# Seven groups instead of four take the first k tile, three of them leave PSUM in turn, and constant matmuls fill two pauses of TensorE

## The chip, the cores and the metric

The kernel runs on one core of a Trainium2 chip. The metric is device time in microseconds (us), and less is better. A profiled execution gives beside its time a span, from the first to the last instruction. The engines are PE (TensorE; PEld is its loading of stationary operands), DVE (VectorE), ACT (ScalarE), POOL (GpSimd) and SP (SyncE, which here issues the weight transfers). Each engine works through its own instructions in a fixed order.

## What is computed

One decoder layer for 256 tokens of width 2048, in float32, with weights that are read once:

```
mod = silu(c) W_ada + b_ada -> shift1, scale1, gate1, shift2, scale2, gate2
h   = RMSNorm(x)(1+scale1)+shift1
p   = h W_in, columns split into [retention q,k,v,g | HGRN2 q,f,i,g | gate A | gate B]
yA  = W_retO( LN_head(Retention(rope(q),rope(k),v)) * silu(g) )
yB  = W_hgO( RMS_head(HGRN2(silu(q), f, i)) * silu(g) )
x   = x + gate1 * ( (sigmoid(gA)*yA + sigmoid(gB)*yB) W_out )
h2  = RMSNorm(x)(1+scale2)+shift2
[a, b] = split(causal_depthwise_conv3(h2 W_up))
out = RMSNorm_final( x + gate2 * ( (silu(a) * b) W_down ) )
```

The change touches the beginning alone: the norm of x, `scale1` and `shift1`, and the first 12 column groups of `p = h W_in`.

## The kernel before

**Products in three parts.** A float32 weight is split into a rounded upper part `wh` (ACT, line 167) and the rest `wl` (DVE, `raw - wh`, line 172), and so are the activations `hT` (the first half of a tile is the upper part, from ACT, line 345; the second half is the rest, from DVE, line 350). PE multiplies upper by upper, upper by rest and rest by upper. There are 12 groups g of 512 columns (`wa[g]`) and 16 k tiles of 128 rows. In this text a **unit** is one k tile of one group: a piece of 128x512 weights, for PE 12 matmuls of 256 columns (`mm_cols`, lines 209 to 211), or 6 of 512 columns (`mm_rows`, lines 196 to 198; groups 4, 5, 10, 11). The whole loop has 192 units. Two units can come in one transfer of 128x1024, and are then split in one instruction each of ACT and DVE.

**The activations come k tile by k tile.** `ada[k]` is a generator that makes `hT` of one k tile: four transfers of `ada1` (0.5 MB each), four dot products on DVE (`ada_dot`, line 398), then the small ACT steps (409, 410, 412), and `modulated`, which writes `hT`. So a group can only be multiplied with the k tiles that are there, and the loop goes round the groups several times. At each visit of a group `have` says how many k tiles there are to be:

```python
have = min(KT, 2 + int((work - LAG) / ADA_EVERY))
```

`work` counts the units that are traced, `ADA_EVERY` is 11.

**PSUM.** Groups 0 and 1 (`RESIDENT`) stay in PSUM (`po` buffers) until they are done. Any other group gets one of two `pg` buffers for a visit, and then leaves it: `take` copies it out with ACT at the group's first visit (`fresh`, line 743), and adds it to what is there with DVE at each later one (line 745). A `pg` buffer is free for the visit after next once that is done.

**Order.** DMA, ACT and DVE instructions of the opening are pinned to the order of the code (`pin`); later the framework orders them, and `pump` mixes in the generators: queue 1 with the `ada` tiles, queue 0 with the HGRN2 and retention work as soon as its groups are done. SP issues the weights in order into 12 `raw` buffers; `wh` and `wl` have four buffers each.

**The beginning.** PE broadcasts `c` (line 259) for its silu, sums the squares of x (`token_rstd`, line 298: matmuls with one column), waits for `1/rms`, broadcasts that (line 312) into `rx`, and waits until the first `hT` is there. Then groups 0 to 3 take k tile 0, and after four more dots k tile 1; groups 2 and 3 leave PSUM, and the loop goes on with group 4.

Of the kernel before, what the change touches and what calls it, by code (L numbers as in the profile page):

```python
# [14 lines left out]
BF16 = mybir.dt.bfloat16  # L15
I32 = mybir.dt.int32
AF = mybir.ActivationFunctionType
ALU = mybir.AluOpType

P = 128  # L20
# [9 lines left out]
G = 512  # L30
NORM_EPS = 1e-6
HEAD_EPS = 1e-5
FIRST = 4
RESIDENT = 2
ADA_EVERY = 11
LAG = 1
NOSYNC = mybir.DependencyInfo(mybir.DependencyClass.NoSync, mybir.DependencyReason.DATA)
SMALL = 70

# [16 lines left out]
class Kernel:  # L56
# [181 lines left out]
    def constants(self):  # L238
        nc, a, c = self.nc, self.a, self.consts
        self.ones = c.tile([P, P], F32, name="ones")  # L240
        nc.vector.memset(self.ones, 1.0)
        self.eps1 = c.tile([P, 1], F32, name="eps1")
        nc.vector.memset(self.eps1, NORM_EPS)
        self.eps2 = c.tile([P, 1], F32, name="eps2")
        nc.vector.memset(self.eps2, HEAD_EPS)
        self.halfpi = c.tile([P, 1], F32, name="halfpi")
        nc.vector.memset(self.halfpi, math.pi / 2)

        self.silu = []
        self.sc = c.tile([P, D + 1], F32, name="sc")  # L250
        nc.vector.memset(self.sc[:, D:], 1.0)
        rows = [self.blk([1, GW], name="crow") for _ in range(2)]
        for u, row in enumerate(rows):
            nc.scalar.dma_start(out=row, in_=a["c"][:, u * GW : (u + 1) * GW])
        self.small_loads(nc.scalar, ("ident", "gn1"))
        for u in range(4):
            at = slice(u * G, (u + 1) * G)
            ps = self.po()
            nc.tensor.matmul(ps, lhsT=self.ones[0:1, :], rhs=rows[u // 2][:, u % 2 * G : (u % 2 + 1) * G], start=True, stop=True)
            self.silu.append((self.sc[:, at], ps))  # L260

    def small_loads(self, engine, names):
        for name in names:
            ap = self.a[name]
            t = self.consts.tile(list(ap.shape), ap.dtype, name=name)
            self.tc.keep_in_program_order(engine.dma_start(out=t, in_=ap))
            setattr(self, name, t)
# [22 lines left out]
    def token_rstd(self, parts):  # L290


        nc = self.nc
        ps = self.po()[:, :NT]
        for i, z in enumerate(parts):
            for t in range(NT):

                nc.tensor.matmul(
                    ps[:, t : t + 1],
                    lhsT=z[:, t * P : (t + 1) * P],  # L300
                    rhs=self.ones[:, 0:1],
                    start=i == t == 0,
                    stop=i == len(parts) - 1,
                    skip_group_check=True,
                )
        q = self.small([P, NT], name="rq")
        nc.scalar.activation(q, ps, AF.Sqrt, bias=self.eps1, scale=1.0 / D)
        self.pin(nc.vector.reciprocal(q, q))

        ps = self.po()[:, :T]  # L310
        for t in range(NT):
            nc.tensor.matmul(ps[:, t * P : (t + 1) * P], lhsT=q[:, t : t + 1].to_broadcast([P, P]), rhs=self.ident, start=True, stop=True)
        return ps

    def sqrt_table(self):
# [393 lines left out]
    def run(self):  # L709
        nc, a = self.nc, self.a  # L710
# [11 lines left out]
        def act(k):  # L722
            return hT[k // 2][:, k % 2, :]

        def ada1(k):
            if k > 0 and k % 2 == 0:
                ins = self.times(k, 2, rx_sb)
                self.tc.add_manual_dep(ins.ins, self.last.ins.name, NOSYNC, reason="behind the weights traced ahead of it")
            yield from self.scale_shift("ada1", k, s1, t1, self.gn1)
            if k % 2 == 0:  # L730
                hT[k // 2] = self.blk([P, 2, 2 * T], F32R, name="hT")
            self.modulated(act(k), self.xT[k // 4][:, k % 4, :], k, s1, t1)
            yield 0.7

        accs = [self.blk([P, NT, G] if c0 in ROWS else [P, 4, T], name="p") for c0 in ATT]
        done = [0] * len(ATT)
        mms = [self.mm_rows if c0 in ROWS else self.mm_cols for c0 in ATT]

        def take(g, ps, fresh):
            for at, z in self.parts(ps, ATT[g] in ROWS):  # L740
                dst = accs[g][:, at, :]
                if fresh:
                    nc.scalar.activation(dst, z, AF.Copy)  # L743
                else:
                    nc.vector.tensor_tensor(dst, dst, z, ALU.add)


        ada = [ada1(k) for k in range(KT)]
        for _ in range(3):
            next(ada[0])  # L750
        rx = self.token_rstd(parts)
        rx_sb = c.tile([P, T], F32, name="rx_sb")
        ps = [self.po2(), self.po2(), self.pg(), self.pg()][:FIRST]
        for k in range(2):
            for i in range(4 if k else 1):
                if k and i == 1:
                    self.times(k, 1, rx)
                next(ada[k])
            if k == 0:
                self.times(k, 1, rx)  # L760

            ahead = 2 * k
            uppers = [self.upper(a["wa"][g][:, k : k + 1, :], 1, G) for g in range(ahead + 1)]
            rests = [self.rest(z) for z in uppers[:ahead]]
            for _ in ada[k]:
                pass
            for g in range(FIRST):
                if g >= ahead:
                    rests.append(self.rest(uppers[g] if g < len(uppers) else self.upper(a["wa"][g][:, k : k + 1, :], 1, G)))
                wh, wl = rests[g]  # L770
                if k == g == 0:
                    self.pin(nc.scalar.activation(rx_sb, rx, AF.Copy))
                mms[g](ps[g], act(k), wh[:, 0, :], wl[:, 0, :], k == 0, k == 1 and g >= RESIDENT)
        for _ in range(2):
            next(ada[2])
        self.ordered = False
        for gen in ada[2:]:
            self.start(gen, 1)
        for g in range(FIRST):
            done[g] = 2  # L780
            if g >= RESIDENT:
                take(g, ps[g], True)
        self.pace(1, 4, ADA_EVERY / 2)
        self.pace(0, 3.5, 24)

        work = 2 * FIRST
        g = FIRST
        att, gates = [], []
        small = False
        while min(done) < KT:  # L790
            if work > SMALL and not small:
# [3 lines left out]
                self.start(self.lower_bound())  # L795
            have = min(KT, 2 + int((work - LAG) / ADA_EVERY))
            m = have - done[g]
            if m > 0:
                self.finish(*ada[:have])
                if g < RESIDENT:  # L800
                    self.products(mms[g], ps[g], a["wa"][g], act, done[g], m, first=False, last=have == KT)
# [14 lines left out]
            g = (g + 1) % len(ATT)  # L816
            if have == KT and done[0] < KT:
                g = min(i for i in range(len(ATT)) if done[i] < KT)
# [9 lines left out]
        for j in range(4):  # L828
            ps = self.rows(a["wb"][j], act)
# [55 lines left out]
        for j in range(4):  # L885
            last = j == 3
            x1.append(self.load_rows(j))
            if not last:
                g = self.row(self.gate["gate1"], j, "g1")
            if j == 2:  # L890
                g3 = self.row(self.gate["gate1"], 3, "g1")
            elif last:
                g = g3
            ps = self.products(self.mm_rows, self.po2() if last else self.pg(), a["wout"][j], actm, 0, KT, hold=4 * last, gain=g if last else None)
            if last:
                g = None
# [13 lines left out]
            if j == 2:  # L910
                part = self.row_part(ss)
# [241 lines left out]
```

## Time and profile before

| what | value |
|---|---|
| time, median of 3 runs (lowest to highest) | 1524.89 us (1524.85 to 1526.18) |
| the profiled execution: its time / its span | 1525.32 us / 1523.5 us |
| PE busy | 1506.1 us, 99% of the span |
| DVE busy | 1207.2 us, 79% |
| ACT busy | 846.1 us, 56% |
| HBM traffic | 252 GB/s over the span; 398 to 417 GB/s in most of the first 60 us |
| mean granted TensorE clock | 0.999 |

The profiled execution lies 0.43 us above the median, within the spread of the three runs. Its time exceeds its span by 1.8 us, which lie before the first and after the last instruction. Busy times are lengths of instructions laid together; a PE that is busy without a gap may still run at half its clock, which the distance from one matmul to the next shows. An idle engine matters where the engine that sets the end waits for it.

### The profile page before, as it was taken

Reading aid. Unit: us, or ns where it says so; the run is one execution under the profiler, and the core shown is the slowest. Engines: PE = TensorE matmul, PEld = TensorE weight load, DVE = VectorE, ACT = ScalarE, POOL = GpSimd, SP = SyncE. Lnnn points to the kernel's source line nnn. Section 1 sums busy time; section 2 is a strip of 40 time slices with the busy share of each in tenths; the row PEclk is TensorE's granted clock in tenths of the full one; section 3 lists DMA queues with packets and bytes.
Section 4 is the critical chain, followed back from the end, with each engine's and each line's share of the span. In section 5 each row is a group of like instructions: output and inputs, shape, how many; then the busy total and the mean of one; then the engine's idle time right before and its main releaser. Section 6 shows DMA issues by size and latency. Waiting matters only on the chain.

```text
span 1523.5 us, 22103 instructions
## 1 busy us (share of the span) xinstructions
PE 1506.1 (99%) x8226; PEld 1301.0 (85%) x8226; DVE 1207.2 (79%) x1640; ACT 846.1 (56%) x1199; POOL 4.0 (0%) x8
## 2 busy tenths in 40 slices
PE   8999999999999999999999999999999999999997
PEld 6999999888888888888888888888888888888886
DVE  7899996997998877898967777778777769455694
ACT  6655445757866554445456555555555558344343
POOL 0000000000000000000000000000000000000000
PEclk9999999999999999999999999999999999999999
DMA  9999997778888789999947777777777766667651
GB/s 374 375 347 331 316 328 221 231 270 263 271 265 264 264 288 322 322 296 349 321 139 229 236 236 231 230 232 233 226 235 236 221 191 191 206 207 212 176 182 56
DMA packets 110993, 385.68 MB, mean 253 GB/s; under 512 B 12803, under 2 KB 13347, under 8 KB 110885
## 3 DMA queue, kind: packets, MB, share of 16 engines
q1 hardware_dynamic: 110016, 383.14, 76.5%
q8 instruction: 64, 1.05, 0.3%
q10 hardware_dynamic: 868, 1.13, 0.2%
q14 instruction: 45, 0.36, 0.1%
HBM read 382.11 MB, written 2.11 MB: 252 GB/s over the span
## 4 chain that ended last, share of the span: by engine, by line
PE 97%; DVE 1%; ACT 1%; DMA 1%; issue 0%; SPq 0%; DVEq 0%; ACTq 0%
PE pg L196 14%; PE pg L197 14%; PE pg L198 14%; PE po L986 11%; PE pg L986 10%; PE po L988 5%; PE pg L988 5%; PE po L196 3%; PE po L198 3%; PE po L197 3%; PE pg L211 3%; PE pg L209 3%; PE pg L210 3%; PE po L209 1%; PE po L210 1%; PE po L211 1%
## 5 line engine op out<-in xcount | busy, mean ns | idle before, releaser
L167 ACT ACTIVATE wh<-raw 128x1024 fp32r<-128x1024 f32 (+1 forms) x536 | 550.8, 1033 | 529.5 <-PE pg L198 170.2
L172 DVE TENSOR_TENSOR wl<-raw,wh 128x1024 fp32r<-128x1024 f32 (+1 forms) x536 | 635.5, 1192 | 246.7 <-ACT wh L167 245.3
L398 DVE SCALAR_TENSOR_TENSOR raw<-raw,sc 128x1024 f32<-128x1024 f32 x192 | 234.1, 1223 | 0.0
L986 PE MATMUL pg<-h2T,wh 128*128 128x512 f32 x704 | 221.7, 396 | 0.6 <-ACT h L380 0.6
L986 PE MATMUL po<-h2T,wh 128*128 128x512 f32 x704 | 221.2, 396 | 0.0
L196 PE MATMUL pg<-wh,hT 128*128 128x512 f32 x512 | 203.0, 397 | 0.2 <-ACT p L743 0.2
L197 PE MATMUL pg<-wl,hT 128*128 128x512 f32 x512 | 199.8, 390 | 0.5 <-DVE wl L172 0.5
L198 PE MATMUL pg<-wh,hT 128*128 128x512 f32 x512 | 199.8, 390 | 0.0
L988 PEld LDWEIGHTS pg<-h2T,wl 128*128 128x128 f32 x704 | 132.3, 188 | 31.6 <-DVE wl L172 0.5
L988 PEld LDWEIGHTS po<-h2T,wl 128*128 128x128 f32 x704 | 132.4, 188 | 31.1
L988 PE MATMUL pg<-h2T,wl 128*128 128x256 f32 x704 | 138.5, 278 | 0.1
L988 PE MATMUL po<-h2T,wl 128*128 128x256 f32 x704 | 138.3, 278 | 0.0
L198 PEld LDWEIGHTS pg<-wh,hT 128*128 128x128 f32 x512 | 96.2, 188 | 20.2
L197 PEld LDWEIGHTS pg<-wl,hT 128*128 128x128 f32 x512 | 96.3, 188 | 19.7 <-DVE wl L172 1.0
L196 PEld LDWEIGHTS pg<-wh,hT 128*128 128x128 f32 x512 | 96.3, 188 | 19.5 <-ACT p L743 0.4
L211 PE MATMUL pg<-hT,wl 128*128 128x256 f32 x384 | 108.9, 284 | 0.6 <-DVE wl L172 0.6
L209 PE MATMUL pg<-hT,wh 128*128 128x256 f32 x384 | 108.9, 284 | 0.1
L210 PE MATMUL pg<-hT,wh 128*128 128x256 f32 x384 | 108.8, 283 | 0.0
L986 PEld LDWEIGHTS pg<-h2T,wh 128*128 128x128 f32 x704 | 107.3, 189 | 0.8 <-ACT h L380 0.8
L986 PEld LDWEIGHTS po<-h2T,wh 128*128 128x128 f32 x704 | 107.2, 189 | 0.0
L211 PEld LDWEIGHTS pg<-hT,wl 128*128 128x128 f32 x384 | 73.8, 192 | 0.8 <-DVE wl L172 0.8
L209 PEld LDWEIGHTS pg<-hT,wh 128*128 128x128 f32 x384 | 73.8, 192 | 0.6 <-ACT wh L167 0.2
(242 smaller groups left out, 2224.7 us busy)
## 6 DMA issues: line engine op xcount, KB each, us to landing
raw<-in_wup SPq DMA_DIRECT2D x176, 512.0 KB, 4.4
raw<-in_wdown SPq DMA_DIRECT2D x88, 512.0 KB, 4.3
raw<-in_wa SPq DMA_DIRECT2D x80, 512.0 KB, 5.9
raw<-in_ada SPq DMA_DIRECT2D x64, 512.5 KB, 5.8
raw<-in_ada SPq DMA_DIRECT2D x64, 512.0 KB, 5.4
raw<-in_wab SPq DMA_DIRECT2D x64, 512.0 KB, 4.9
raw<-in_gate SPq DMA_DIRECT2D x32, 512.5 KB, 4.5
raw<-in_wb SPq DMA_DIRECT2D x32, 512.0 KB, 4.9
```

Of the source, the lines that this page charges most:

```text
L167: self.pin(self.nc.scalar.activation(wh, raw, AF.Copy))
L172: self.last = self.nc.vector.tensor_tensor(wl, raw, wh.bitcast(F32), ALU.subtract)
L196: nc.tensor.matmul(ps[t], lhsT=hi, rhs=wh, start=first, stop=False)
L197: nc.tensor.matmul(ps[t], lhsT=hi, rhs=wl, start=False, stop=False)
L198: nc.tensor.matmul(ps[t], lhsT=lo, rhs=wh, start=False, stop=last)
L209: nc.tensor.matmul(out, lhsT=wh[:, cs], rhs=hi, start=opens, stop=False, skip_group_check=True)
L210: nc.tensor.matmul(out, lhsT=wh[:, cs], rhs=lo, start=False, stop=False, skip_group_check=True)
L211: nc.tensor.matmul(out, lhsT=wl[:, cs], rhs=hi, start=False, stop=last, skip_group_check=True)
L398: dot = self.pin(nc.vector.scalar_tensor_tensor(raw[:, 0, :], raw[:, 0, :], 1.0, self.sc[:, u * GW : u * GW + w], ALU.mult, ALU.mult, accu ...
L986: self.pin(nc.tensor.matmul(ps[j + z], lhsT=wh[:, cs[z]], rhs=act, start=kt == 0, stop=False))
L988: nc.tensor.matmul(ps[j + z][:, :T], lhsT=wl[:, cs[z]], rhs=act[:, :T], start=False, stop=kt == KT - 1)
```

## The change

The first k tile is taken by seven groups, in the order 4, 5, 0, 6, 1, 2, 3, instead of four. Groups 4, 5 and 6 stop at one k tile and leave PSUM at once, with an ACT copy, each before a later group is begun that needs its buffer; group 2 and 3 stay for k tile 1 as before. The dots of k tile 1 stand between the groups instead of behind them. `work` starts at 11 units in place of 8, the loop goes on with group 7, and `LAG` is 5 in place of 1. Two times three matmuls with constant operands (bfloat16, 128x512, into a `pg` buffer that nobody reads) stand behind the sum of squares and behind the broadcast of `1/rms`, and the matmuls there are pinned.

```diff
 FIRST = 4
+EXTRA = 3
-LAG = 1
+LAG = 5
...
+        self.busy = self.sb.tile([P, G], BF16, name="busy", tag="k1", bufs=7)
+        nc.gpsimd.memset(self.busy, 1.0)
+        self.spare = self.pg()[0]
...
+    def keep_busy(self, ps, n):
+        for _ in range(n):
+            self.pin(self.nc.tensor.matmul(ps, lhsT=self.busy[:, :P], rhs=self.busy, start=True, stop=True))
...
+        self.keep_busy(self.spare, 3)
         q = self.small([P, NT], name="rq")
...
+        self.keep_busy(self.spare, 3)
         return ps
...
-        ps = [self.po2(), self.po2(), self.pg(), self.pg()][:FIRST]
-        for k in range(2):
-            for i in range(4 if k else 1):
-                if k and i == 1:
-                    self.times(k, 1, rx)
-                next(ada[k])
...
+        order = [4, 5, 0, 6, 1, 2, 3]
+        leave = {3: 4, 5: 5, 6: 6}
+        next(ada[0])
+        self.times(0, 1, rx)
+        part = one(order[0], 0)
+        for _ in ada[0]:
+            pass
+        for i, g in enumerate(order):
+            wh, wl = self.rest(one(g, 0) if i else part)
+            if i in leave:
+                take(leave[i], ps[leave[i]], True)
+            if i == 0:
+                self.pin(nc.scalar.activation(rx_sb, rx, AF.Copy))
+            ps[g] = self.po2() if g < RESIDENT else self.pg()
+            mms[g](ps[g], act(0), wh[:, 0, :], wl[:, 0, :], True, g >= FIRST)
+            done[g] = 1
+            if i == 1:
+                self.times(1, 1, rx)
+            if i >= 3:
+                next(ada[1])
...
-        work = 2 * FIRST
-        g = FIRST
+        work = 2 * FIRST + EXTRA
+        g = FIRST + EXTRA
```

**What it moves.** Counted over the whole program, DVE gets 12 more adds of line 745 (49 in place of 37), because the loop visits groups with fewer new k tiles each; and 8 splits of 128x1024 become 16 of 128x512, on ACT, on DVE and as transfers. PE gets the six constant matmuls.

In the opening, DVE's order before, from the rest of the first `hT` tile to that of the second (`wl` are splits, `dot` the dots of `ada[1]`):

```order
L350 TENSOR_TENSOR hT_186<-h_187,hT_186 128x256
L172 TENSOR_TENSOR wl_183<-raw_180,wh_182 128x512
...
L172 TENSOR_TENSOR wl_244<-raw_241,wh_243 128x512
L398 SCALAR_TENSOR_TENSOR raw_260,dot_259<-raw_260,sc 128x1024
L388 TENSOR_TENSOR xT_95<-xT_95,po_166 128x256
...
L398 SCALAR_TENSOR_TENSOR raw_273,dot_269<-raw_273,sc 128x1025
L172 TENSOR_TENSOR wl_279<-raw_276,wh_278 128x512
L172 TENSOR_TENSOR wl_284<-raw_281,wh_283 128x512
L350 TENSOR_TENSOR hT_186<-h_294,hT_186 128x256
```

And DVE's order now, over the same stretch:

```order
L361 TENSOR_TENSOR hT_189<-h_190,hT_189 128x256
L173 TENSOR_TENSOR wl_186<-raw_183,wh_185 128x512
L173 TENSOR_TENSOR wl_206<-raw_203,wh_205 128x512
L399 TENSOR_TENSOR xT_98<-xT_98,po_172 128x256
...
L173 TENSOR_TENSOR wl_240<-raw_237,wh_239 128x512
L409 SCALAR_TENSOR_TENSOR raw_258,dot_257<-raw_258,sc 128x1024
L173 TENSOR_TENSOR wl_264<-raw_261,wh_263 128x512
...
L409 SCALAR_TENSOR_TENSOR raw_330,dot_306<-raw_330,sc 128x1025
L173 TENSOR_TENSOR wl_336<-raw_333,wh_335 128x512
L173 TENSOR_TENSOR wl_341<-raw_338,wh_340 128x512
L361 TENSOR_TENSOR hT_189<-h_351,hT_189 128x256
```

The four dots, which stood together behind four splits, now alternate with the splits of the fifth, sixth and seventh group; nine splits, four dots and one product with `rx` stand between the two `hT` rows.

ACT's order now, just behind the opening (`p_134`, `p_135` and `p_139` are the copies of groups 2, 3 and 7 out of PSUM, `wh_461` and `wh_496` the upper parts for groups 8 and 9):

```order
L168 ACTIVATE wh_423<-raw_421 128x1024
L754 ACTIVATE p_134<-pg_291 128x1024
L420 ACTIVATE s_128<-dot_411 128x1
L754 ACTIVATE p_135<-pg_317 128x1024
L421 ACTIVATE s_128<-gn_88,s_128 128x1
L168 ACTIVATE wh_461<-raw_459 128x1024
L754 ACTIVATE p_139<-pg_420 128x1024
L168 ACTIVATE wh_496<-raw_494 128x1024
```

And ACT's order before at the same place (`p_131` to `p_133` are groups 2, 3 and 4, `wh_392` and `wh_421` the upper parts for groups 5 and 6):

```order
L167 ACTIVATE wh_366<-raw_364 128x1024
...
L743 ACTIVATE p_131<-pg_174 128x1024
L167 ACTIVATE wh_392<-raw_390 128x1024
L743 ACTIVATE p_132<-pg_175 128x1024
L743 ACTIVATE p_133<-pg_363 128x1024
L412 ACTIVATE t_126<-dot_384 128x1
L167 ACTIVATE wh_421<-raw_419 128x1024
```

Each upper part still stands behind a copy that waits for PE to finish a group.

At the end of the loop, DVE's order now, where groups 5 to 10 have their last visits (`p_137` to `p_142` are their adds, `b` the scans of the first HGRN2 head block, `wl_3338` the first split of the next stage):

```order
L756 TENSOR_TENSOR p_137<-p_137,pg_3183 128x1024
L173 TENSOR_TENSOR wl_3299<-raw_3296,wh_3298 128x512
L526 SCALAR_TENSOR_TENSOR b_3204<-ones,f_3202 128x128 x5
L756 TENSOR_TENSOR p_138<-p_138,pg_3207 128x1024
L526 SCALAR_TENSOR_TENSOR b_3204<-ones,f_3202 128x128 x3
L539 TENSOR_TENSOR ke_3497<-b_3204 128x512
L173 TENSOR_TENSOR wl_3319<-raw_3316,wh_3318 128x512
L756 TENSOR_TENSOR p_139<-p_139,pg_3241 128x1024
L756 TENSOR_TENSOR p_140<-p_140,pg_3275 128x1024
L173 TENSOR_TENSOR wl_3338<-raw_3335,wh_3337 128x1024
L756 TENSOR_TENSOR p_141<-p_141,pg_3295 128x1024
L756 TENSOR_TENSOR p_142<-p_142,pg_3315 128x1024
```

And DVE's order before at its end of the loop (`p_135` to `p_137` are the adds of groups 6 to 8; the splits behind them belong to visits of 5 and 4 units):

```order
L172 TENSOR_TENSOR wl_3142<-raw_3139,wh_3141 128x512
L745 TENSOR_TENSOR p_135<-p_135,pg_3096 128x1024
L745 TENSOR_TENSOR p_136<-p_136,pg_3118 128x1024
L172 TENSOR_TENSOR wl_3162<-raw_3159,wh_3161 128x1024
L745 TENSOR_TENSOR p_137<-p_137,pg_3138 128x1024
L172 TENSOR_TENSOR wl_3182<-raw_3179,wh_3181 128x1024
L172 TENSOR_TENSOR wl_3201<-raw_3198,wh_3200 128x512
L172 TENSOR_TENSOR wl_3215<-raw_3212,wh_3214 128x1024
```

The last visits, which were three of one unit each and then long ones, are now all short (three of two units, three of one), and the adds of six groups and the first scans stand close together there.

## Rows read from the trace of the kernel before

**Rows 1.** The page: the engines' busy time, share of the span, instructions.
```profile
PE 1506.1 (99%) x8226; PEld 1301.0 (85%) x8226; DVE 1207.2 (79%) x1640; ACT 846.1 (56%) x1199; POOL 4.0 (0%) x8
```
**Rows 2.** Busy us (instructions) by stretch: PE, PEld, DVE, ACT, POOL; then clock, DMA.
```profile
17.00:25.00 8.00, 7.70 (x48) 7.49 (x48) 7.89 (x15) 4.22 (x10) 0.00 (x0) 1.00 1.04 406
25.00:40.00 15.00, 13.01 (x80) 11.45 (x81) 12.30 (x19) 10.79 (x18) 0.00 (x0) 1.00 1.03 406
40.00:60.00 20.00, 20.00 (x154) 19.38 (x154) 15.37 (x22) 14.88 (x21) 0.00 (x0) 1.00 1.03 410
60.00:90.00 30.00, 30.00 (x196) 27.55 (x195) 26.23 (x36) 16.34 (x25) 0.00 (x0) 1.00 0.95 342
90.00:152.00 62.00, 62.00 (x439) 58.37 (x438) 60.82 (x90) 34.27 (x50) 0.96 (x1) 1.00 0.96 334
```
**Rows 3.** The timeline, PE, opening: start us, length us, instructions [idle before <-who ended it].
```profile
17.13 0.80 PE L209 MATMUL po<-hT,wh 128*128 128x256 f32 x2 [1.20 <-ACT hT L345]
20.75 0.38 PE L210 MATMUL po<-hT,wh 128*128 128x256 f32 x1
20.96 0.28 PE L211 MATMUL po<-hT,wl 128*128 128x256 f32 x1
22.39 0.28 PE L211 MATMUL pg<-hT,wl 128*128 128x256 f32 x1
22.51 0.28 PE L209 MATMUL pg<-hT,wh 128*128 128x256 f32 x1
26.00 0.74 PE L209 MATMUL po<-hT,wh 128*128 128x256 f32 x4 [1.17 <-ACT hT L345]
39.23 0.39 PE L211 MATMUL pg<-hT,wl 128*128 128x256 f32 x1 [0.55 <-DVE wl L172]
```
**Rows 4.** The timeline, DVE, from the first k tile on.
```profile
17.11 0.43 DVE L350 TENSOR_TENSOR hT<-h,hT 128x256 fp32r<-128x256 f32 x1 [0.19 <-ACT hT L345]
...
24.78 0.09 DVE L398 DVE_READ_ACCUMULATOR raw<-raw,sc 128x1 f32 x1
...
26.47 0.43 DVE L350 TENSOR_TENSOR hT<-h,hT 128x256 fp32r<-128x256 f32 x1 [0.40 <-ACT h L349]
...
28.02 0.69 DVE L388 TENSOR_TENSOR xT<-xT,rx_sb 128x512 f32<-128x512 f32 x1
28.62 1.22 DVE L398 SCALAR_TENSOR_TENSOR raw<-raw,sc 128x1024 f32<-128x1024 f32 x1
29.76 0.09 DVE L398 DVE_READ_ACCUMULATOR raw<-raw,sc 128x1 f32 x1
```
**Rows 5.** Groups by line and shape, DVE, 17 to 152 us: count | busy us, mean ns | idle before.
```profile
L172 DVE TENSOR_TENSOR wl<-raw,wh 128x1024 fp32r<-128x1024 f32 x37 | 45.0, 1222 | 8.8 <-ACT wh L167 8.7
...
L745 DVE TENSOR_TENSOR p<-p,pg 128x1024 f32<-128x1024 f32 x13 | 15.9, 1220 | 2.1 <-PE pg L211 2.1
L172 DVE TENSOR_TENSOR wl<-raw,wh 128x512 fp32r<-128x512 f32 x20 | 13.3, 686 | 0.1
```
**Rows 6.** Who waited for whom, 25 to 60 us: us, times, longest.
```profile
DVE wl L172 <- ACT wh L167: 6.9, 6, 1.5
```
**Rows 7.** The timeline, ACT: a copy out of PSUM, and the split behind it.
```profile
35.76 1.03 ACT L743 ACTIVATE p<-pg 128x1024 f32<-128x1024 f32 x1 [0.81 <-PE pg L198]
...
36.87 1.05 ACT L167 ACTIVATE wh<-raw 128x1024 fp32r<-128x1024 f32 x1
```
**Rows 8.** The timeline, two places where PE comes to a split: PEld's and PE's rows.
```profile
119.77 0.19 PEld L197 LDWEIGHTS pg<-wl,hT 128*128 128x128 f32 x1 [0.17 <-DVE wl L172]
...
152.41 0.39 PE L197 MATMUL pg<-wl,hT 128*128 128x512 f32 x1
...
152.64 0.39 PE L198 MATMUL pg<-wh,hT 128*128 128x512 f32 x1
```
**Rows 9.** The timeline, the end of the loop: PE's wait, and DVE's scans.
```profile
282.80 0.51 PE L197 MATMUL pg<-wl,hT 128*128 128x512 f32 x1 [0.48 <-DVE wl L172]
287.91 2.63 DVE L515 TENSOR_TENSOR_SCAN b<-ones,f 128x128 f32<-128x128 f32 x8
```

More of the change, by code (lines that the diff above doesn't have):

```diff
@@ L296, in token_rstd @@
             for t in range(NT):
-                nc.tensor.matmul(
+                self.pin(nc.tensor.matmul(
                     ps[:, t : t + 1],
@@ L304, in token_rstd @@
                     skip_group_check=True,
-                )
+                ))
+        self.keep_busy(self.spare, 3)
         q = self.small([P, NT], name="rq")
@@ L311, in token_rstd @@
         for t in range(NT):
-            nc.tensor.matmul(ps[:, t * P : (t + 1) * P], lhsT=q[:, t : t + 1].to_broadcast([P, P]), rhs=self.ident, start=True, stop=True)
+            self.pin(nc.tensor.matmul(ps[:, t * P : (t + 1) * P], lhsT=q[:, t : t + 1].to_broadcast([P, P]), rhs=self.ident, start=True, stop=True))
+        self.keep_busy(self.spare, 3)
         return ps
@@ L752, in run @@
         rx_sb = c.tile([P, T], F32, name="rx_sb")
-        ps = [self.po2(), self.po2(), self.pg(), self.pg()][:FIRST]
-        for k in range(2):
-            for i in range(4 if k else 1):
-                if k and i == 1:
-                    self.times(k, 1, rx)
-                next(ada[k])
[L759 to L773, printed above, removed]
+        ps = [None] * (FIRST + EXTRA)
@@ new lines, in one @@
+        def one(g, k):
+            return self.upper(a["wa"][g][:, k : k + 1, :], 1, G)
+        order = [4, 5, 0, 6, 1, 2, 3]
[18 more added lines that the diff above has]
+                next(ada[1])
@@ L774, in run @@
+        ahead = 2
+        uppers = [one(g, 1) for g in range(ahead + 1)]
+        rests = [self.rest(z) for z in uppers[:ahead]]
+        for _ in ada[1]:
+            pass
+        for g in range(FIRST):
+            if g >= ahead:
+                rests.append(self.rest(uppers[g] if g < len(uppers) else one(g, 1)))
+            wh, wl = rests[g]
+            mms[g](ps[g], act(1), wh[:, 0, :], wl[:, 0, :], False, g >= RESIDENT)
+            done[g] = 2
         for _ in range(2):
@@ L778, in run @@
             self.start(gen, 1)
[L779 to L782, printed above, removed]
+        for g in range(RESIDENT, FIRST):
+            take(g, ps[g], True)
         self.pace(1, 4, ADA_EVERY / 2)
         self.pace(0, 3.5, 24)
-        work = 2 * FIRST
-        g = FIRST
+        work = 2 * FIRST + EXTRA
+        g = FIRST + EXTRA
         att, gates = [], []
```

## Prediction

> **What bounds the kernel now.** I read the page's busy line first: PE is busy 99% of the span, DVE 79% [rows 1]. So DVE as a whole is no bound, and only places where PE stands still or runs slowly can give time. The table by stretch says where these lie [rows 2]: PE is full from 40 us on, and lacks 0.3 us of 17 to 25 and 2.0 us of 25 to 40. But the same table shows that DVE is not idle beside it: 60.82 of the 62.00 us from 90 to 152. What PE wins in the opening, it keeps only if DVE comes along.
>
> [...] And PE stands 1.17 us before the second `hT`, 0.55 us for a `wl` at 39.23 [rows 3], and twice some 0.2 us between these.
>
> I measure a **lateness** L: the time at which PE reaches a matmul, less 0.12 us for each matmul of 256 columns and 0.227 for each of 512 that it had to do before. At the start L = 17.1. At 152.41 us, 720 and 193 such matmuls lie behind it, 130.2 us, so L = 22.2; 0.23 is the step there [rows 8]. [...] From 152 to 278 us PE makes no such pause; at the end of the loop it makes some, the largest of 0.48 for a `wl` [rows 9], and L rises there by an estimated 1.25. Behind that DVE has its surplus and PE is gap-free. **So the change is worth what it does to L at 152 us, and at the end of the loop.**
>
> **DVE's side.** A split or add of 128x1024 lasts 1.22 us and one of 128x512 0.686 [rows 5], but they overlap: a dot begins at 28.62 and its last row at 29.76, and the 512-wide product begins at 28.02, 0.60 before it [rows 4]. So I count 1.14, 0.60, 1.13 for an add. From 17 to 152 us DVE is busy 122.6 of 135 us and idle 12.4: 0.1, 2.7, 4.6, 3.8 and 1.2 in the five stretches [rows 2]. 8.7 of that it waits for a `wh` of ACT [rows 5]. At 119.77 PE waits 0.17 us for a `wl` [rows 8]: the two engines are level there.
>
> **The change, part by part.**
>
> *Three more groups on the first k tile.* Seven units have 84 matmuls of 256 columns, 9.9 us, in place of 48, from 17.13 to some 27.6 with a slow start. The second `hT` is later than before: its last dot ends at 24.78, its rest begins at 26.47, 1.7 later [rows 4]; three more splits of 0.60 put the dot to 26.6 and the rest to 28.4. PE, which waited 1.17 us, now waits some 0.6. With a faster start that makes L = 18.0 behind the second `hT`, and 18.7 behind the next pause (below).
>
> *Constant matmuls.* If they raise the clock before 17.13, the 1.7 us of slow steps shrink to a start of 0.6. They stand in pauses, so cost PE nothing that anything waits for; if they delay the broadcast of `1/rms` by one of them, that is 0.2 to 0.4 us. I take nothing.
>
> *Twelve more adds, sixteen halves for eight wholes.* Up to the split of the unit 97 (which PE reaches after 768 and 188 matmuls, 134.8 us), DVE now has 31 splits x 1.14 + 35 x 0.60 = 56.3; 37 dots x 1.14 = 42.2; 22 adds x 1.13 = 24.9; products and `hT` rests 6.7; small ones 2.7: 132.8 us. That is 9 adds and 9 splits more than before (13 adds, 37 and 20 splits [rows 5]). It is ready at 17.1 + 132.8 and some 0.3 for the hand-over, 150.2, plus its idle time. PE with L = 18.7 is there at 153.5. So **idle time of up to 3.3 us leaves the whole gain of 3.5; idle time of 6.8 takes all of it**; before it was 12.4.
>
> *How much idle is left?* The adds fill some of it, since they are ready when DVE waits. But what makes it wait stays: a `wh` that stands on ACT behind a copy, and the copy behind the end of a visit on PE. Before, DVE waited so six times, 6.9 us, from 25 to 60 us [rows 6]; the copy at 35.76 waits 0.81 for PE, lasts 1.03, and the 1.05 of the split follow [rows 7]. In the new order each of the upper parts for groups 8 to 11 still stands behind such a copy. PE ends the second unit of group 3 at about 33.8 (four units of 1.44 from 28.0, where the upper half of `hT` is there); copy 1.0, small step 0.4, split 0.95, rest 1.14 make 37.5, while DVE was free at 35.7: 1.9 us of idle with the hand-over, and a pause of 0.7 for PE (L = 18.7). The same chain at the next groups gives 0.25, 0.7, 1.35 and 0.6; the first second visit waits 1.5 behind the copy of group 11, and one add 0.4 for PE. Sum 6.7. DVE is ready at 156.9, L = 22.1. **Head: -0.1, say -0.2 us**, since early adds may fill a little of it.
>
> By the rows PE has no way around DVE here. [...]
>
> *The end of the loop.* Before, DVE's burst there is one of long visits. Now from the end of group 5 on DVE has five adds 5.7, splits 0.6 + 0.6 + 1.14, a product 0.6 and eight scans; these last 2.63 together [rows 9]: 11.2 us, against 10.0 us of matmuls that PE has until the next stage needs a `pg` buffer. That makes 1.5 us, and 0.5 at the split behind it, 2.0 in place of 1.25: **+0.75**. With the scans later, nothing; with all of them ahead, +1.5.
>
> **Sum.** -0.2 + 0.75 = +0.55: the profiled 1525.32 becomes 1525.85, and on the median, 0.43 lower, **1525.4 us**.
>
> **The rivals.**
>
> *The gain is kept (faster).* DVE's idle shrinks to 3.3 us or less, because the adds stand exactly where it waited. Then L falls from 22.2 to 18.7 at 152 us, -3.5, and with the end between 0 and +0.75 the time is 1521.4 to 1522.2. For it: nine adds and nine splits more in the same 135 us leave DVE little idle if PE is to keep its pace. Against it: seven in ten of the idle microseconds wait for a `wh` of ACT [rows 5], and an add behind such a wait in DVE's order fills nothing.
>
> *DVE is the bound and waits as before (slower).* DVE's order is fixed; if the idle stays at 9.5 to 12.4, it is ready at 159.7 to 162.6, L is 24.9 to 27.8, the price 2.7 to 5.6, with the end 3.4 to 6.3: 1528 to 1531. It decides from an idle time of 9.1 on, where the sum passes 3 us. Against it: 4.6 of the 12.4 lie between 40 and 60 us [rows 2], where the new visits already have adds.
>
> *The constant matmuls change nothing in the clock.* The start is as slow as before, PE ends the seven units 1.1 us later, the copies and with them the `wh` come 0.8 later: 1526.2. For it: PE stands 1.20 us before 17.13 for `hT` [rows 3], after the last of them, and six matmuls are few. [...]
>
> **How the numbers follow.** A measurement of this kernel tells about 0.2%, 3 us, from no change. Forecast (1523 to 1527.5): 0.48. Clock unchanged (around 1526.2): 0.18. Gain kept: 0.18. DVE waits as before: 0.16. Faster by over 3 us needs under 1521.8: two thirds of the third case, where the end costs little, 0.12, and 0.05 from cases in which PE's pauses in the opening shrink by more than I count: 0.17. Slower, over 1528.0: the fourth case without its lower edge, 0.15. The rest, 0.68, is within. The range 1521.4 to 1528.8 leaves out the far part of the fourth case (0.10) and a tenth at the other end.
>
> **What would show it.** Steps of 0.12 from 17.5 us on show the constant matmuls right; 0.21 until 20 or later show them wrong. L at 41 us should be 18.7, and DVE 98 to 100% busy from 60 to 150 us with PE's waits for `wl` of line 173 in the same stretch, until L is 22; an L that stays at 18.7 beyond 150 us shows the gain kept. DVE's waits for `wh` between 33 and 60 us should sum to some 6 us. Around 278 us PE should lose 2 us by waits for `pg` and `wl`. The stages behind should last as before. The prediction fails if DVE's idle up to 150 us is under 4 or over 9 us, or if a part that I cost at nothing (POOL's memset, the broadcast of `1/rms`) moves 17.13 by over 1 us.

## The result: slower, by waits of TensorE, most of which the sum had placed but mis-sized

The changed kernel takes 1529.42 us (median of 7 runs, 1528.66 to 1531.89), the kernel before 1525.58 in the same rounds (7 runs, 1524.85 to 1526.34): a ratio of 1.0028, interval 1.0019 to 1.0038. That is 3.8 us, 0.28%, slower; the forecast was 1525.4 with a range of 1521.4 to 1528.8. The profiled execution took 1530.22 us with a span of 1528.4, 0.8 above its median.

The page's busy line of the changed kernel answers to [rows 1]: PE is 4.0 us longer busy and DVE 12.4 us, near what twelve adds of 1.13 us make.

```profile
PE 1510.1 (99%) x8232; PEld 1299.4 (85%) x8232; DVE 1219.6 (80%) x1660; ACT 844.8 (55%) x1204; POOL 4.6 (0%) x9
```

The table by stretch of the changed kernel answers to [rows 2] (columns as there); the last row is one stretch more.

```profile
17.00:25.00 8.00, 8.00 (x43) 6.21 (x42) 7.61 (x15) 5.90 (x11) 0.00 (x0) 1.00 1.03 401
25.00:40.00 15.00, 13.99 (x113) 13.38 (x112) 12.60 (x20) 10.82 (x18) 0.00 (x0) 1.00 1.03 405
40.00:60.00 20.00, 19.89 (x131) 18.20 (x131) 15.99 (x23) 15.75 (x25) 0.00 (x0) 1.00 1.00 365
60.00:90.00 30.00, 29.37 (x192) 26.51 (x191) 29.73 (x38) 13.56 (x20) 0.00 (x0) 1.00 0.96 326
90.00:152.00 62.00, 61.36 (x449) 58.32 (x448) 61.37 (x87) 33.87 (x52) 0.96 (x1) 1.00 0.93 318
152.00:200.00 48.00, 47.26 (x319) 43.53 (x318) 47.98 (x69) 24.90 (x38) 0.00 (x0) 1.00 0.95 332
```

PE has gained in 25 to 40 us (13.99 busy in place of 13.01) and is no longer full from 40 us on. From 60 us on DVE is full, or nearly: 29.73 of 30, 61.37 of 62, 47.98 of 48 us. ACT is half idle beside it.

The timeline of PE in the changed kernel, answering to [rows 3] and [rows 8]: the first products, the second `hT` (29.52), and the pauses behind.

```profile
18.00 1.58 PE L197 MATMUL pg<-wh,hT 128*128 128x512 f32 x2
...
21.28 0.39 PE L198 MATMUL pg<-wl,hT 128*128 128x512 f32 x1
21.51 0.39 PE L199 MATMUL pg<-wh,hT 128*128 128x512 f32 x1
...
29.52 0.74 PE L210 MATMUL po<-hT,wh 128*128 128x256 f32 x4 [0.43 <-ACT hT L356]
...
39.48 0.39 PE L212 MATMUL pg<-hT,wl 128*128 128x256 f32 x1 [0.48 <-DVE wl L173]
...
64.33 0.50 PE L198 MATMUL pg<-wl,hT 128*128 128x512 f32 x1 [0.45 <-DVE wl L173]
...
129.72 0.50 PE L198 MATMUL pg<-wl,hT 128*128 128x512 f32 x1 [0.64 <-DVE wl L173]
...
159.21 0.50 PE L198 MATMUL pg<-wl,hT 128*128 128x512 f32 x1 [0.74 <-DVE wl L173]
...
294.35 0.36 PE L210 MATMUL pg<-hT,wh 128*128 128x256 f32 x1 [0.95 <-DVE p L756]
...
387.95 0.50 PE L198 MATMUL pg<-wl,hT 128*128 128x512 f32 x1 [0.76 <-DVE wl L173]
```

The early products follow each other by 0.23 us per 512 columns (21.28 to 21.51), where those of before took 0.21 per 256 until 20.96 [rows 3], and the second `hT` costs 0.43 in place of 1.17. Behind that the pauses are for a `wl`, but for two at the end of the loop that are for an add, which frees the `pg` buffer: the one at 294.35 and one of 0.3 us. The last row lies in the next stage, where the kernel before has no pause. A row's idle time leaves out the tail of the matmul ahead, so what a pause costs shows better in the distance of two matmuls (0.76 us of idle at 387.95, but 1.26 from the matmul ahead).

I sum that up by the lateness L of the prediction, here with steps of 0.1197 and 0.2268 us (256 and 512 columns): L at the first product, and what it gains in the opening (the first 36 us of matmuls), in the loop (to 250 us of them) and at its end (to 280 us). The mean steps between 60 and 280 us are a trifle longer, 0.1201 and 0.2274 in the kernel before, which alone makes the 0.5 in its loop.

| profiled execution | start | opening | loop | end |
|---|---|---|---|---|
| before | 17.13 | +5.1 | +0.5 | +1.3 |
| changed | 18.00 | +2.9 | +4.2 | +2.3 |
| difference | +0.9 | -2.2 | +3.7 | +1.0 |

These make 3.3 to 3.4 of the 4.9 us between the two profiled executions; 1.3 more lie at 387 us, where the step from one matmul to the next is 1.26 us in place of 0.23, and the steps on either side are 0.1 longer. From the first product with `h2T`, in the second half of the layer (783.01 us before, 787.89 now), to the end both take the same, 740.5 us. The start differs from run to run: the profiled executions of the eight kernels here that have the same opening have it between 16.62 and 18.76 us, and this one is 0.9 us above the median. DVE's rows (the kernel before first, then the changed one) show that the constant matmuls are not the cause, since the first dot is late already, ahead of them:

```profile
11.07 1.22 DVE L398 SCALAR_TENSOR_TENSOR raw<-raw,sc 128x1024 f32<-128x1024 f32 x1
...
11.93 1.22 DVE L409 SCALAR_TENSOR_TENSOR raw<-raw,sc 128x1024 f32<-128x1024 f32 x1
```

From there to the first product it is 6.06 us before and 6.07 now. So of the 3.8 us between the medians, opening -2.2, loop +3.7, end +1.0 and next stage +1.3. This is an account by one execution of each kernel. In the five that share these seven groups, the constant matmuls and a LAG of 3 or more, and differ in the loop, the first 24 us of matmuls cost 2.5 to 2.8 us, and 3.8 in a sixth (run 8, where steps of 0.43 per 512 columns last until 22.3 us), so the opening's part differs from one execution to the next, mostly by a few tenths.

### The profile page after: what moved, and what is told of

Read it like the earlier page. It is cut to its first block, busy times and chain, and to the rows that moved or that the text cites. A ratio compares the mean times of both kernels' runs of the same rounds, so it can differ in the third digit from the quotient of the medians.

```text
span 1528.4 us, 22183 instructions
## 1 busy us (share of the span) xinstructions
PE 1510.1 (99%) x8232; PEld 1299.4 (85%) x8232; DVE 1219.6 (80%) x1660; ACT 844.8 (55%) x1204; POOL 4.6 (0%) x9
## 3 DMA queue, kind: packets, MB, share of 16 engines
q10 hardware_dynamic: 868, 1.13, 0.2%
## 4 chain that ended last, share of the span: by engine, by line
PE 92%; DVE 3%; DMA 2%; ACT 1%; issue 1%; SPq 0%; DVEq 0%; ACTq 0%
PE pg L198 13%; PE pg L197 13%; PE pg L199 13%; PE po L1011 11%; PE pg L1011 10%; PE po L1013 5%; PE pg L1013 5%; PE po L198 3%; PE po L199 3%; PE po L197 3%; PE pg L212 2%; PE pg L211 2%; PE pg L210 2%; DVE wl L173 1%; PE po L211 1%; PE po L212 1%
## 5 line engine op out<-in xcount | busy, mean ns | idle before, releaser
L197 PEld LDWEIGHTS pg<-wh,hT 128*128 128x128 f32 x512 | 96.5, 188 | 21.5 <-ACT wh L168 1.6
L199 PEld LDWEIGHTS pg<-wh,hT 128*128 128x128 f32 x512 | 96.2, 188 | 20.3
```

The source lines that it names most:

```text
L197: nc.tensor.matmul(ps[t], lhsT=hi, rhs=wh, start=first, stop=False)
L199: nc.tensor.matmul(ps[t], lhsT=lo, rhs=wh, start=False, stop=last)
```

## The experiments

Theory A: from 60 to 200 us DVE is full, and what the twelve adds take there beyond its idle time comes back as PE's waits for `wl`. Theory B: the loss is the start, constant matmuls included. Theory C: it is the order of the work behind the loop. Theory D came up after the first four runs. Times are medians; the ratio to the kernel before of the same rounds stands with its interval.

**1. Fewer adds by a sooner loop.**

```diff
-LAG = 5
+LAG = 1
```

> The changed kernel with LAG back at 1: the seven groups and the constant matmuls stay, but the loop's visits ask for more k tiles each, which makes 40 adds out of PSUM in place of 49 (before: 37). Theory A (DVE is full in the loop, and the adds beyond its idle time come back as waits of PE for wl): nine adds of 1.13 us less, 10 us of DVE work, so the waits of PE between 40 and 200 us (3.7 us in the changed kernel) shrink to under 1.5 and the time falls from 1529.4 to 1525.5 to 1527. Theory B (the loss is the start, where the first product begins 0.87 us later behind the constant matmuls, and the slow first steps): no change, 1528.7 to 1530. Theory C (the loss is in the order of the work behind the loop, where PE waits 1.3 us near 388 us): still 1528.5 or more.

Measured: 1525.33, ratio 0.9999 (0.9990 to 1.0008). In the trace the opening costs 3.7, the loop 1.8 in place of 4.2, and near 388 us PE waits for nothing. The loss is gone with the seven groups and the constant matmuls in place, so B falls. A and C are not told apart, since both waits went.

**2. Without the constant matmuls.**

```diff
-        for _ in range(n):
+        for _ in range(0):
             self.pin(self.nc.tensor.matmul(ps, lhsT=self.busy[:, :P], rhs=self.busy, start=True, stop=True))
```

> The changed kernel without its six constant matmuls, all else as it is. [...] Theory B: the first product begins at 17.1 again in place of 18.0 and the time is 0.5 to 1 us lower, 1528.4 to 1528.9.

Measured: 1531.33, ratio 1.0035 (1.0023 to 1.0048): by the medians 1.9 us slower than with them, though the intervals of the two ratios overlap. Theory A had 1529.4 to 1530.2, most of PE's delay being hidden behind DVE, and theory B 1528.4 to 1528.9: both missed that. PE's timeline in this run shows steps of 0.43 us per 512 columns, and 0.21 per 256 until after 23 us:

```profile
20.34 0.63 PE L199 MATMUL pg<-wh,hT 128*128 128x512 f32 x1
20.76 0.63 PE L198 MATMUL pg<-wl,hT 128*128 128x512 f32 x1
21.19 0.63 PE L199 MATMUL pg<-wh,hT 128*128 128x512 f32 x1
```

The opening costs 5.1 (with them 2.9), the loop the same 4.2, its end the same 2.3. So 2.2 us lost in the opening are not hidden behind DVE: from 25 to 60 us DVE waits 6.0 us for `wh` in place of 4.8, ACT's copies wait 6.5 us for PE in place of 5.3, and all three move back together.

**3. The sooner loop of before made later.**

```diff
-LAG = 1
+LAG = 5
```

> The kernel before with LAG at 5 alone: four groups in the opening and no constant matmuls, but 45 adds out of PSUM in place of 37. Theory A: eight adds more are 9 us of DVE work in the loop; DVE had 12.4 us idle up to 152 us, of which 8.7 waits for wh that no add fills, so PE waits for wl and the time is 1.5 to 4 us above the kernel before: 1527 to 1529.5. Theory B and theory C: within 0.7 us of before, 1525 to 1526.3.

Measured: 1527.18, ratio 1.0012 (1.0003 to 1.0021). The loop costs 3.5 in place of 0.5, its end 0.2 in place of 1.3. PE's largest new wait, from PE's timeline (the other, 0.64 us at 275.61, is for an add):

```profile
156.34 0.38 PE L211 MATMUL po<-hT,wl 128*128 128x256 f32 x1 [1.50 <-DVE wl L172]
```

DVE is busy 35.74 of the 36 us up to there, from 120 to 156. That is theory A on the kernel before, without the opening.

**4. Fewer adds by longer visits.**

```diff
-            if m > 0:
+            if m >= 3 or m > 0 and (have == KT or done[g] == 0):
```

> The changed kernel with LAG 5, but a group is passed over until at least three new k tiles are there for it (first and last visits excepted): 30 adds in place of 49. Theory A: 19 adds less, 21 us of DVE work, so PE waits for no wl between 60 and 200 us and the 1.4 us that the opening wins at 36 us of matmuls are kept: 1523 to 1525. Theory B: 1528.7 to 1530. Theory C: 1528 or more, if the ends of the loop are as crowded.

Measured: 1528.93, ratio 1.0023 (1.0014 to 1.0032), no clear difference from the changed kernel. The expectation had the edit wrong: the trace has 37 adds of line 756, not 30, so 12 less than the changed kernel and as many as the kernel before. All the theories missed or gave a wrong reason: 12 adds less, and the loop costs 4.7. Each group passed over adds 0.5 to `work`, so the next k tiles were asked for sooner, and their four dots of 1.14 us each had to be done sooner: by 90 us DVE has begun 27 dots and 8 adds, in the changed kernel 23 and 9. It is full up to there and idle for 4 us in the 30 behind; from 120 to 152 it is full again, 31.76 of 32. The first two of these stretches of its table:

```profile
60.00:90.00 30.00, 28.79 (x196) 26.03 (x195) 30.00 (x42) 15.54 (x26) 0.00 (x0) 1.00 0.97 351
90.00:120.00 30.00, 30.00 (x233) 29.12 (x232) 25.89 (x39) 15.28 (x22) 0.96 (x1) 1.00 0.96 342
```

Theory D: when the dots are asked for decides, not the adds.

**5. The price of the adds alone.** A against D.

```diff
+        adds = [0]
...
-                    nc.vector.tensor_tensor(dst, dst, z, ALU.add)
+                    adds[0] += 1
+                    if adds[0] % 4:
+                        nc.vector.tensor_tensor(dst, dst, z, ALU.add)
```

> The changed kernel with every fourth add out of PSUM left out (12 of 49; the sums lack those pieces), so that DVE has as many adds as before, while the visits, the dots and the order of all other work stay. Theory A (the price is the time of the added adds on a full DVE): PE's waits between 60 and 200 us, 3.4 us, go, and the time falls by 2.5 to 3.4 us to 1526 to 1527. Theory D (not the adds, but when the visits ask for the dots of the next k tiles, decides; the run with 30 adds was no faster): at most 1 us less, 1528.4 to 1529.4. Both leave the 1.3 us near 388 us as they are.

Measured: 1526.5, ratio 1.0010 (1.0001 to 1.0019): 2.9 us less than the changed kernel. The loop costs 3.0 in place of 4.2, its end 0.9 in place of 2.3. So the adds do cost, 0.24 us each of their 1.13. An add left out also frees its `pg` buffer sooner, and the gain at the end, where PE had waited for one, may be that in part.

**6. The same cost put into the kernel before.**

```diff
+        adds = [0]
...
-                    nc.vector.tensor_tensor(dst, dst, z, ALU.add)
+                    adds[0] += 1
+                    for _ in range(1 if adds[0] % 3 else 2):
+                        nc.vector.tensor_tensor(dst, dst, z, ALU.add)
```

> The kernel before with every third add out of PSUM made twice (12 more; the sums take those pieces twice), nothing else changed: the suspected cost alone. Theory A: 13.6 us more of DVE work in the loop, of which its idle time before 152 us takes only a part: 1527.5 to 1530. Theory D: within 0.9 us of before, 1524.7 to 1526.2.

Measured: 1530.74, ratio 1.0037 (1.0025 to 1.0050), 5.3 us slower, 0.44 each. The loop costs 3.4 in place of 0.5, its end 3.5 in place of 1.3. The table from 60 to 200 us, of this kernel:

```profile
60.00:200.00 140.00, 137.79 (x955) 128.94 (x954) 135.49 (x181) 73.87 (x106) 1.91 (x2) 1.00 0.92 320
```

PE lacks 2.2 us there, where it lacked none up to 152 us before [rows 2], and DVE, busy 135.49, is still idle for 4.5. PE waits before DVE is full over the whole stretch: what it lacks lies between 90 and 152 us, where DVE is busy 61.68 of 62, and its waits there are for `wl` (1.8 and 0.4 us), not for a buffer. A holds; D as the only cause falls.

**7. The constant matmuls alone.** The changed lines of `constants`, `keep_busy` and `token_rstd` in the kernel before. The changed kernel gains 1.9 us by these matmuls, by the medians of run 2; the question here is whether four groups gain by them too.

```diff
...
+        self.keep_busy(self.spare, 3)
         q = self.small([P, NT], name="rq")
...
+        self.keep_busy(self.spare, 3)
         return ps
```

> The kernel before with the six constant matmuls alone. [...] If that gain belongs to the matmuls themselves: steps of 0.12 from some 18 us on, and 1523 to 1524.2. If it needs the seven groups (the second hT is not there earlier, so four groups only wait longer for it): a longer wait at the second hT and 1524.8 to 1525.6.

Measured: 1525.51, ratio 1.0000 (0.9991 to 1.0009). The steps are 0.12 us per 256 columns from 18.5 us on (0.21 until 20.96 before [rows 3]), and the time goes into the wait for the second `hT`:

```profile
25.67 0.74 PE L209 MATMUL po<-hT,wh 128*128 128x256 f32 x4 [2.10 <-ACT hT L355]
```

It was 1.17 us [rows 3]. With four groups the shorter steps are worth nothing, with seven 1.9 us; and without the constants the seven groups' opening costs 5.1 (run 2), as much as that of the kernel before. Each part of the change needs the other.

**8. The next stage.**

```diff
         self.pace(0, 143.0, 88)
+        self.credit[0] = -5
```

> The changed kernel with the credit of queue 0 set to -5 where the next stage begins: the loop is untouched, and behind it the steps of the HGRN2 blocks stand some steps later, so that ACT's order near 388 us has an upper part wh between the sigmoid and the square root in place of none. Theory C (1.8 us of the loss were only the place where function tables and gates meet on ACT): the wait of 1.0 us for a wl near 388 us goes, 1527.6 to 1528.5. If the wait only moves to another place: 1529 to 1529.8.

Measured: 1527.82, ratio 1.0019 (1.0010 to 1.0027), by the medians 1.6 us less than the changed kernel, though the intervals overlap. First the place in the changed kernel, from the timelines of ACT and (last row) DVE:

```profile
375.06 1.04 ACT L168 ACTIVATE wh<-raw 128x1024 fp32r<-128x1024 f32 x1
...
380.29 1.06 ACT L508 ACTIVATE f<-p 128x1024 f32<-128x1024 f32 x1
...
383.60 1.28 ACT L282 ACT_TABLE_LOAD   x1
384.89 0.30 ACT L282 ACTIVATE rsh<-ssh,eps 128x4 f32<-128x4 f32 x1
385.10 0.59 ACT L512 ACTIVATE f<-f,lb,lb 128x256 f32<-128x256 f32 x1
385.59 1.04 ACT L168 ACTIVATE wh<-raw 128x1024 fp32r<-128x1024 f32 x1
...
386.67 1.23 DVE L173 TENSOR_TENSOR wl<-raw,wh 128x1024 fp32r<-128x1024 f32 x1
```

From 376.10 to 385.59 ACT makes no `wh`: between two of them stand a silu, the sigmoid, its four small steps, four squares, three table loads of 1.28 us each and the square root. The same place on ACT in this run:

```profile
382.94 1.28 ACT L282 ACT_TABLE_LOAD   x1
384.23 0.30 ACT L282 ACTIVATE rsh<-ssh,eps 128x4 f32<-128x4 f32 x1
384.44 1.04 ACT L168 ACTIVATE wh<-raw 128x1024 fp32r<-128x1024 f32 x1
385.50 1.28 ACT L508 ACT_TABLE_LOAD   x1
```

An upper part stands between the two tables, and PE waits for nothing from 370 to 400 us. The loop and its end cost the same 4.2 and 2.3 as in the changed kernel, and behind them the profiled execution of this run is 1.2 us shorter. So C holds for this part of the loss: the changed loop shifted the steps of the next stage against its weights.

**9. LAG at -1, in the changed kernel.** 36 adds.

```diff
-LAG = 5
+LAG = -1
```

> The changed kernel with LAG at -1: 36 adds (LAG 1: 40, LAG 5: 49), and each k tile is asked for two units, some 2.9 us, sooner than with LAG 1. If only the number of adds counts: DVE has 4.5 us less work than with LAG 1, no wait of PE for wl stays between 60 and 200 us, 1523.5 to 1524.8. If the dots, which now have to be done sooner, press DVE as hard in the first 60 us: 1525.3 to 1527, with PE's waits for wl before 60 us instead.

Measured: 1528.89, ratio 1.0022 (1.0013 to 1.0030). The fewest adds of the three values under 5, and 3.6 us slower than with LAG 1. PE's timeline:

```profile
38.72 0.39 PE L210 MATMUL pg<-hT,wh 128*128 128x256 f32 x1 [2.32 <-ACT wh L168]
...
39.98 0.39 PE L212 MATMUL pg<-hT,wl 128*128 128x256 f32 x1 [0.76 <-DVE wl L173]
...
41.40 0.41 PE L210 MATMUL pg<-hT,wh 128*128 128x256 f32 x1
41.61 0.41 PE L211 MATMUL pg<-hT,wh 128*128 128x256 f32 x1
```

The sooner dots hold up the first visits behind the opening: it costs 7.8. The upper part that PE waits for begins on ACT at 37.62, behind two copies and the small steps of the next k tile, the last of which begins at 37.44, after DVE's last dot of it (37.24). And behind the two pauses of 2.3 and 0.8 us the steps are long again (0.21 us per 256 columns in place of 0.12, from 41.2 to 44.4 us). Theory D holds on this side.

**10. The kernel before with the constant matmuls and LAG at -1.** 33 adds.

```diff
-LAG = 1
+LAG = -1
...
+        self.keep_busy(self.spare, 3)
         q = self.small([P, NT], name="rq")
```

> The kernel before with the constant matmuls and LAG at -1: 33 adds in place of 37. With four groups in the opening DVE had 4.6 us idle from 40 to 60 us, so the sooner dots have room: if the adds at the end of the loop cost PE its 1.3 us there, 1524.3 to 1525.3; if nothing in the loop bounds PE with 37 adds, as its waits say, no change, 1525.0 to 1525.9; if the sooner dots are too soon, over 1526.

Measured: 1525.49, ratio 0.9998 (0.9990 to 1.0007). The end of the loop costs 0.05 in place of 1.3, the opening 5.9 in place of 5.1 and the loop 0.9 in place of 0.5: what the end gave back, the sooner dots took.

**11. LAG at 3, in the changed kernel.** 42 adds.

```diff
-LAG = 5
+LAG = 3
```

> The changed kernel with LAG at 3: 42 adds. By the number of adds it lies near LAG 1: 1525.3 to 1526.8. If the places where the steps of the next stage fall decide as much as the adds, as near 388 us, up to 1528.

Measured: 1526.21, ratio 1.0003 (0.9994 to 1.0012). The opening costs 4.9 (a wait of 1.3 us for a `wh` behind it), the loop 1.8, its end 0.05. So LAG at -1, 1, 3 and 5 gives 1528.9, 1525.3, 1526.2 and 1529.4: a valley between two costs, dots that are asked for too soon, and visits that are so short that they need more adds. Which of 1 and 3 is better these times do not tell: their intervals overlap.

**12. What the opening is worth where DVE has room.**

```diff
+        adds = [0]
...
-                    nc.vector.tensor_tensor(dst, dst, z, ALU.add)
+                    adds[0] += 1
+                    if adds[0] % 2:
+                        nc.vector.tensor_tensor(dst, dst, z, ALU.add)
...
         self.pace(0, 143.0, 88)
+        self.credit[0] = -5
```

> The changed kernel with every second add out of PSUM left out (24 of 49; the sums lack those pieces) and the credit of queue 0 at -5 as in the run on the next stage: what the opening is worth where DVE has room. If the opening wins its 2 us against before and only DVE and ACT take them back: no wait of PE for wl from 60 to 200 us, 1522.8 to 1524.3, under the kernel before. If the loop with more and shorter visits loses by something else too (copies, pg buffers, hT): 1525 or more, with waits that do not name a wl.

Measured: 1523.03, ratio 0.9985 (0.9976 to 0.9994). The table from 60 to 200 us of this kernel:

```profile
60.00:200.00 140.00, 140.00 (x986) 131.79 (x985) 126.48 (x179) 74.45 (x112) 0.96 (x1) 1.00 0.97 338
```

With DVE at 126.48 of 140 us (139.09 in the changed kernel) PE is full. The opening costs 2.6 in place of 5.1, so it won 2.5, near the 2.3 us between the medians; the start (+0.2), the loop (+0.6), its end (-0.7) and what lies behind (+0.5) almost cancel out. It leaves work out and is no version to keep; of the versions that compute all, none beats the kernel before.

## Why the prediction was wrong

**The bound, and where it would show.** Right. PE's pauses behind the second `hT` and up to 160 us are for `wl` of line 173, DVE is 99 to 100% busy from 60 to 200 us, and runs 5 and 6 moved the time with DVE's adds alone. The gain was expected to be taken back there, and was.

**The opening, "-3.5".** Half right. The short steps came early, as forecast: 0.23 us per 512 columns from 19.67 us on, where before it was 0.12 per 256 from 20.96 on. The constant matmuls cost nothing at the start: the ten profiled executions with them begin the first product at 16.62 to 18.76 us (median 16.9), the four without at 17.00 to 17.43, and the late ones are late before them. When the short steps begin differs from run to run: 1.2 to 3.8 us after the first product in the ten with them, 3.8 to 6.5 in the four without. But the opening won 2.2, not 3.5. The 0.6 us to which 1.7 us of slow steps were to shrink was the author's estimate, and no run shows it: before, 17 matmuls took the 3.83 us from 17.13 to 20.96, 1.8 more than 17 steps of 0.12; the first three products now, of 512 columns, take 1.7 us (18.00 to 19.67), 1.0 more than three steps of 0.2268. And one split ahead of the second `hT` waited 0.70 us for its `wh`. The rival that the constant matmuls change nothing was wrong, and was mispriced: they are worth 1.9 us here by the medians of run 2 (2.2 in the opening of its trace), not 0.8, since DVE does not hide PE's delays but waits along with them (6.0 us for `wh` in run 2, 4.8 in the changed kernel). From 20.3 to 21.5 us the step per 512 columns is 0.43 us in run 2 and 0.23 in the changed kernel.

**The step that failed first: "DVE is ready at 156.9".** DVE was to have 132.8 us of work and 6.7 of idle time up to the split of unit 97, and PE to be there at L = 22.1. In the trace the wait of PE for that split ends at 159.21. Of the 2.3 us between, 0.9 are the start; the idle time was 7.4 (from 17.97 to 159.15, laid together) and the work 133.8, with the very 31 and 35 splits and 22 adds that were counted; the hand-over took 0.2 less than the 0.3 allowed. So neither term was off by more than a us, 1% of the work; but the answer is the difference of two sums of some 135 us, and a step of 1 us on either changes its sign. The waits for `wh`, forecast as 6 us between 33 and 60 us, were 4.8 in six waits in the changed kernel's list of waits from 25 to 60 us, of which one of 0.70 lies ahead of 33, so 4.1; a wait of 1.3 for an `hT` of ACT stands beside them:

```profile
DVE wl L173 <- ACT wh L168: 4.8, 6, 1.4
```

They were 6.9 in [rows 6]. Counted by PE's terms the miss is the same 1.7 us: the opening won 1.3 less, and the waits took 3.7 in place of 3.3. So the head came out 1.5 us slower and not 0.2 faster. The slower rival had DVE's idle time at 9.1 us or more; its outcome came without its condition.

**The price of the adds.** The runs put it between nothing and the whole of their time: 12 adds cost 2.9 us (run 5) or 5.3 us (run 6), of 13.6.

**The end of the loop, "+0.75".** Right in place and nearly in size: +1.0, with a pause for an add's `pg` buffer, as forecast.

**The step that was left out: "the stages behind should last as before".** They did not: 1.3 us in the trace, 1.6 in run 8. The loop's end decides how many pieces of the next stage's weights are traced before each step of an HGRN2 block, and there ACT's order fell badly. Nothing in the sum looked at it. With the 1.5 of the head and 1.0 at the end it makes the 3.8 us.

Not settled: how the 3.7 us of the loop divide between the adds and the time at which the dots are asked for, and why run 5 keeps 3.0 us in the loop with as many adds as before. Its DVE timeline has a wait for an `ada` transfer,

```profile
144.59 1.23 DVE L173 TENSOR_TENSOR wl<-raw,wh 128x1024 fp32r<-128x1024 f32 x1 [2.24 <-DMA raw<-in_ada]
```

and from there DVE works without a pause until PE stands 1.10 us for a `wl` at 156.53; but run 12 has such a wait too (1.90 at 142.33), and no pause of PE behind it. That the gains of runs 5 and 8 add up is shown only by run 12, which takes away more adds than both.

## What to carry to other kernels

Where two engines run level, the gain of one is a small difference of two long sums: give such a forecast the width of 1% of the sums, and look for the engine that will be full, not for the one that waits now. A parameter that sets how late a loop asks for its inputs has a price on both sides (here more partial sums out of PSUM, or dots too soon), so read it as a valley and try both sides. And when a stage's work is shifted against the next one's, look at the order of the slow single steps there (here three loads of function tables at 1.28 us each, and the gates) before costing it at nothing.

## What the hardware showed unexpectedly

After pauses of 2.3 and 0.8 us PE kept its steps of 0.12 us per 256 columns for another 1.2 us, and only then took 0.21 for 3.2 us (run 9). The table by stretch shows that fall in the column of the granted clock, 0.64 from 40 to 44 us; with 1.2 of these 4 us at 1.00, the 2.8 us of long steps ran at an estimated 0.49:

```profile
36.00:40.00 4.00, 0.93 (x7) 0.52 (x5) 2.62 (x6) 3.97 (x9) 0.00 (x0) 1.00 1.03 405
40.00:44.00 4.00, 4.00 (x23) 4.00 (x24) 4.00 (x6) 1.64 (x3) 0.00 (x0) 0.64 1.04 412
```

It does not show the slow steps of the opening, where it reads 1.00 [rows 2] beside steps of 0.21 [rows 3]: in this opening the step has to be read, not the column. That the steps there are a lower clock too is the author's reading of their length, which is that of run 9.
